# Two more Strassen pairs in the second feed-forward half, with weight sums made in DRAM by transfers

## The chip, the cores and the metric

The kernel runs on one core of a Trainium2 chip. The metric is the device time of one execution in microseconds (us), as the median of three runs. Five engines work side by side, each through its own queue in order: PE (TensorE, matmuls; PEld is its weight load), DVE (VectorE), ACT (ScalarE), POOL (GpSimd) and SP (SyncE, which here only issues transfers). Weights come from DRAM by transfers that share 16 DMA engines.

## The reference

One decoder layer on 512 tokens of width 1024, in float32: a feed-forward half, a mixer (attention beside a state-space model), and a second feed-forward half. What the change touches is the last of these, with an inner width of 2816:

```python
def rms_norm(x, g):
    xf = x.astype(jnp.float32)
    y = xf * lax.rsqrt(jnp.mean(xf * xf, axis=-1, keepdims=True) + NORM_EPS)
    return (y * g.astype(jnp.float32)).astype(x.dtype)

def swiglu(x, w_in, w_out):
    gate, up = jnp.split(x @ w_in, 2, axis=-1)
    return (jax.nn.silu(gate) * up) @ w_out

h = rms_norm(x, ffn1_pre_g[l])
x = x + 0.5 * rms_norm(swiglu(h, ffn1_w_in[l], ffn1_w_out[l]), ffn1_post_g[l])
...
h = rms_norm(x, ffn2_pre_g[l])
x = x + 0.5 * rms_norm(swiglu(h, ffn2_w_in[l], ffn2_w_out[l]), ffn2_post_g[l])
```

The factor of `rms_norm` for one token (called r below) is a scalar per token. So r may be applied before or after the product with `w_in`.

## The kernel before, in words

**Precision.** Each float32 operand is split into a high half (`xh`, `whi`, `ah`; made by ACT, L117, L163, L166) and a low half (`xl`, `wlo`, `al`; the difference, made by DVE or POOL, L119, L164, L167). Each product is three matmuls, high by high, high by low, low by high (`mm3`; all matmuls are recorded on L144).

**Tiles of the inner width.** 2816 is 22 tiles f of 128. Each f has a gate tile and an up tile, each a product of 1024x128 weights with 1024x512 inputs. A *standard* f (`products`) takes 2 x 8 x 3 = 48 matmuls of 128x512, tiles `gu`. A *pair* (`pair`, two neighbouring f at once) sees the weights as four blocks a11, a12, a21, a22 (a first index of 2 is the up part, a second index of 2 is the second half of the 1024 rows), and the inputs as four blocks of 4 x 256 columns. Seven products of 24 matmuls of 128x256 give what eight would give (the scheme of Strassen and Winograd). It needs four sums of weight blocks, c3 = a11 + a21, c2 = c3 + a22, c1 = a21 + a22 and c4 = c2 + a12, made by DVE (L609), and sums of input blocks, n1, n2, t3, t4, made once. The products go into the banks `wx`, `wy`, `wq`.

`NSTD` says how many f of each half are standard: 8 in the first half, 6 in the second. Of the 6, the first two (tiles `first`) are computed in the boundary.

**Weights.** SP issues each load (`wraw`, `wa`, `wx`; 512 KB), ACT makes the high half, DVE or POOL the low half. Three `wraw` buffers and four buffers for each half rotate.

**Boundary.** Between two stages `boundary` applies the norm to the residual x. It goes by token halves h = 0, 1: the last products of the stage before (`yt`), then `prep(h, k)` for each of eight row tiles (new x, its `xh` and `xl`, and the square, which POOL adds to `acc`, L178), and `begin(h, k)`, the first matmuls of the next stage (tile `first`). PE sums the squares of the first token half over partitions with `st` in the middle of the second half's `begin`, and of the second half later, in the next stage (`late`); DVE makes `nv` from it and POOL the power r (L207). The first boundary leads from feed-forward to the mixer, the second from the mixer to the second feed-forward half.

**Second half before.** `swiglu_half`: f = 2 to 5 are standard, with eight token transposes of x spread between their matmuls (`xt`, L505, copied out of PSUM by ACT on L507 and stored to DRAM for the end). The input blocks are scaled by the gain and r (L533, 16 ops), then summed and split (`sums`). Eight pairs follow, f = 6 to 20, with the output products `outp` between them; `finish` ends with the last output products and the last norm, tile by tile.

**Order.** Matmuls, transfers marked by `dma` and operations marked by `fix` keep the order of the program. The rest is ordered by the scheduler of the framework on each engine's queue. Semaphores hold an instruction until its operands are ready, and everything behind it on the same engine waits too.

Of the kernel before, what the change touches and what calls it, by code (L numbers as in the profile page):

```python
# [17 lines left out]
P = 128  # L18
# [11 lines left out]
NSTD = (8, 6)  # L30
# [14 lines left out]
class Layer:  # L45
# [30 lines left out]


# [195 lines left out]
    def boundary(self, y, tail, ipost, half, inext, chunks):  # L273
# [40 lines left out]
        def prep(h, k, fix=lambda i: i):  # L314
# [5 lines left out]
            self.split(xh(k)[:, hs[h]], xl(k)[:, hs[h]], xk, self.g(inext, k), fix)  # L320
            self.sq_acc(acc2[:, hs[h]], xk, k == 0, nc.gpsimd)
# [46 lines left out]
        for k in range(KD):  # L368
            if k > 1:
                prep(0, k, fx if k > 5 else lambda i: i)  # L370
            begin(0, k)
            if k == 2:
                post[1][0](late, fix=fx)
            if k == 4:
                rr[1] = post[1][1]()
        for k in range(KD):
            prep(1, k)
            begin(1, k)
            if k == 3:
                pre[0][0](fixp=fx)  # L380
            if k == 6:
                pre[0][1]()
        self.xh, self.xl = xh, xl
# [6 lines left out]
    def ffn(self, n, first, scope):  # L390
# [42 lines left out]
        def outp(i, ms=range(KD), tails=None, hold=0):  # L433
# [3 lines left out]
            def part(m, k0, k1):  # L437
# [15 lines left out]
                else:  # L453
                    nc.vector.tensor_tensor(out=y(m), in0=b[m], in1=y(m), op=ALU.add)
# [20 lines left out]
        prep = sums(True)  # L475
# [5 lines left out]
        for m in range(2, KD):  # L481
# [3 lines left out]
            outp(0, (m,))  # L485
        for f in range(NSTD[0], NF, 2):
# [24 lines left out]
    def seven(self, fin, w_in, ig, r, ah, al):  # L511
# [13 lines left out]
        def sums(early=False):  # L525
# [13 lines left out]
            more[0] = (yield) or fin  # L539
            if early:  # L540
                self.pad(more[0], 192)
# [4 lines left out]
            bh, bl = [self.b16(n, F32R) for n in ("bh", "bl")] if early else (None, None)  # L546
            v = lambda t, i: t.rearrange("p (q k) c -> p q (k c)", q=4)[:, i]

            def plain(*ts):
                for t in ts:  # L550
                    i = len(blocks)
                    blocks.append((v(bh, i), v(bl, i)))
                    self.split(*blocks[i], t)

            if early:
                plain(b11)
            V.scalar_tensor_tensor(out=n2, in0=n1, scalar=-1.0, in1=b22, op0=ALU.mult, op1=ALU.subtract)
            if early:
                plain(b21)
# [6 lines left out]
            if early:  # L566
                plain(b22, n1)
# [4 lines left out]
            if not early:  # L572
                yield
                bh, bl = [self.b16(n, F32R) for n in ("bh", "bl")]
                plain(b11, b21, b22, n1)
            yield

        def block(f, up, kh):
            if up:
                t = wx() if kh else more[0].tile([P, 1024], F32, name="wa", tag="wa")  # L580
# [6 lines left out]
        def cut(t, pool=False):  # L587
            hi, lo = self.halves(True)
# [3 lines left out]
        def times(bank, w, xb, first, parted=False):  # L592
            for g in range(2):
# [914 lines left out]
```

## Time and profile before

| What | Value |
|---|---|
| runs, us | 918.75, 918.01, 916.20 (median 918.01) |
| profiled execution, us | 916.19 |
| its span, us | 914.2 |
| PE busy | 98% of the span |
| DVE busy | 72% |
| ACT busy | 48% |
| POOL busy | 24% |
| the 16 DMA engines, main queue | 34.5% |

Busy shares are means over stages that differ. Matmul ends are modelled in the records, so the time of one matmul is read from start to start. A row of groups gives busy time, then the mean of one in ns, then the idle time of the engine ahead of it and what ended that. A row of the timeline gives start, duration, engine, line and operation, output and inputs, form and count, and in brackets the wait ahead of it.

### The profile page before, as it was taken

The numbers are of one execution on the slowest core, as the hardware profiler recorded it, in microseconds if no ns is written. First come the engines' busy times: TensorE is split into PE (matmuls) and PEld (weight loads), VectorE is DVE, ScalarE is ACT, GpSimd is POOL, SyncE is SP. The second block draws the span as 40 slices with busy tenths as digits, with TensorE's granted clock in tenths as the row PEclk, the third lists the DMA queues.
The fourth block names the chain that finished last, engine by engine and source line by source line (L and its number), as shares of the span: only waits on it lengthen the run. The fifth ranks groups of instructions, "written<-read, shape, count | busy, mean of one in ns | idle before, by whom it ended". The sixth has DMA issues, their size and how long they took to land.

```text
span 914.2 us, 15367 instructions
## 1 busy us (share of the span) xinstructions
PE 898.9 (98%) x6169; PEld 801.4 (88%) x6169; DVE 656.0 (72%) x1071; ACT 442.0 (48%) x685; POOL 217.5 (24%) x127
## 2 busy tenths in 40 slices
PE   9999999999999999999999999999999999999996
PEld 7787789998999989978777889888899989998995
DVE  6999786755678666758898567898368557855756
ACT  6263763553355543525745654573355514541542
POOL 0423301322123134500000025523222222221321
PEclk9999999999999999999999999999999999999999
DMA  8223662334231262283321452145222422332222
GB/s 277 94 70 115 196 248 76 107 102 137 77 119 61 68 194 86 92 221 109 116 70 51 153 167 71 29 179 180 97 93 99 133 92 93 116 116 92 92 93 92
DMA packets 47734, 106.81 MB, mean 117 GB/s; under 512 B 7824, under 2 KB 11152, under 8 KB 47120
## 3 DMA queue, kind: packets, MB, share of 16 engines
q1 hardware_dynamic: 46080, 102.21, 34.5%
q10 hardware_dynamic: 1584, 3.63, 1.1%
q8 instruction: 48, 0.79, 0.3%
q14 instruction: 22, 0.18, 0.1%
HBM read 96.13 MB, written 9.70 MB: 116 GB/s over the span
## 4 chain that ended last, share of the span: by engine, by line
PE 79%; DVE 6%; issue 2%; DMA 2%; ACT 1%; POOLq 0%; POOL 0%; DVEq 0%; SPq 0%; ACTq 0%
PE yo L144 21%; PE wx L144 18%; PE wq L144 9%; PE yt L144 6%; PE wy L144 4%; PE gu L144 4%; PE prj L144 4%; PE first L144 3%; PE prv L144 2%; PE mo L144 2%; PE ys L144 1%; PE st L144 1%; DMA w1d<-w1s 1%; PE pt L1098 1%; PE sc L144 1%
## 5 line engine op out<-in xcount | busy, mean ns | idle before, releaser
L117 ACT CAST whi<-wraw 128x1024 fp32r<-128x1024 f32 (+5 forms) x128 | 124.0, 976 | 160.3 <-PE yo L144 65.5
L119 POOL TENSOR_TENSOR wlo<-wraw,whi 128x1024 fp32r<-128x1024 f32 (+1 forms) x41 | 109.2, 2666 | 297.6 <-ACT whi L117 290.3
L119 DVE TENSOR_TENSOR wlo<-wraw,whi 128x1024 fp32r<-128x1024 f32 (+5 forms) x87 | 107.4, 1242 | 75.7 <-ACT whi L117 75.6
L144 PE MATMUL wx<-tq,whi 128*128 128x256 f32 x720 | 124.7, 276 | 0.0
L144 PEld LDWEIGHTS wx<-tq,whi 128*128 128x128 f32 x720 | 108.3, 188 | 0.0
L119 DVE TENSOR_TENSOR wlo<-wsum,whi 128x1024 fp32r<-128x1024 f32 x60 | 73.6, 1227 | 46.5 <-ACT whi L117 46.4
L117 ACT CAST whi<-wsum 128x1024 fp32r<-128x1024 f32 x60 | 63.0, 1050 | 81.8 <-PE yo L144 28.1
L144 PE MATMUL wx<-tq,wlo 128*128 128x256 f32 x360 | 99.4, 276 | 0.0
L119 POOL TENSOR_TENSOR wlo<-wx,whi 128x1024 fp32r<-128x1024 f32 x15 | 41.5, 2764 | 176.3 <-ACT whi L117 128.5
L144 PEld LDWEIGHTS wx<-tq,wlo 128*128 128x128 f32 x360 | 67.6, 188 | 0.0
L144 PE MATMUL gu<-xh,whi 128*128 128x512 f32 x168 | 67.2, 400 | 0.0
L144 PE MATMUL gu<-xh,wlo 128*128 128x512 f32 x168 | 65.7, 391 | 1.1 <-POOL wlo L119 1.1
L144 PE MATMUL wq<-bh,whi 128*128 128x256 f32 x240 | 66.2, 276 | 0.0
L144 PE MATMUL wq<-bl,whi 128*128 128x256 f32 x240 | 66.2, 276 | 0.0
L144 PE MATMUL wq<-bh,wlo 128*128 128x256 f32 x240 | 66.2, 276 | 0.0
L144 PE MATMUL gu<-xl,whi 128*128 128x512 f32 x168 | 65.5, 390 | 0.0
L144 PE MATMUL yo<-ah,whi 128*128 128x512 f32 x144 | 56.3, 391 | 0.0
L144 PE MATMUL yo<-al,whi 128*128 128x512 f32 x144 | 56.1, 389 | 0.0
L144 PE MATMUL yo<-wlo,ah 128*128 128x512 f32 x144 | 56.0, 389 | 0.0
L144 PE MATMUL yo<-whi,ah 128*128 128x512 f32 x144 | 56.0, 389 | 0.0
L144 PE MATMUL yo<-ah,wlo 128*128 128x512 f32 x144 | 56.0, 389 | 0.0
L144 PE MATMUL yo<-whi,al 128*128 128x512 f32 x144 | 56.0, 389 | 0.0
(267 smaller groups left out, 2385.0 us busy)
## 6 DMA issues: line engine op xcount, KB each, us to landing
wraw<-w1i SPq DMA_DIRECT2D x28, 512.0 KB, 3.7
wraw<-w2i SPq DMA_DIRECT2D x28, 512.0 KB, 3.6
wraw<-w2o SPq DMA_DIRECT2D x18, 512.0 KB, 3.7
wraw<-wmi SPq DMA_DIRECT2D x12, 512.0 KB, 4.1
wraw<-w1o SPq DMA_DIRECT2D x8, 512.0 KB, 4.2
wa<-w2i SPq DMA_DIRECT2D x8, 512.0 KB, 3.7
wx<-w2i SPq DMA_DIRECT2D x8, 512.0 KB, 4.0
wa<-w1i SPq DMA_DIRECT2D x7, 512.0 KB, 3.6
```

The costliest lines, as they stand in the source:

```text
L117: fix(self.nc.scalar.copy(out=hi, in_=raw))
L119: fix(eng.tensor_tensor(out=lo, in0=raw, in1=hi.bitcast(F32), op=ALU.subtract))
L144: i = self.nc.tensor.matmul(*a, **k)
L1098: self.fix(nc.tensor.transpose(b[i][:, o:o + P], sc[:, c:c + P], self.ident))
```

## The change

- `NSTD` of the second half goes from 6 to 2: f = 2 to 5 become two more pairs, so ten pairs run, f = 2 to 20.
- The sums of weight blocks of these ten pairs no longer come from DVE. `block_sums` makes them in DRAM: for each pair two copies of blocks, two accumulating transfers (c3, c1), a copy of c3 to c2, an accumulate, a copy of c2 to c4, an accumulate. Copies are issued by SP, accumulates by POOL, each 512 KB, 80 in all. A step of it is taken by `self.more()` at places in the first half: after standard f, between output products, six in each pair, and eight in the first boundary. A pair of the second half then loads seven blocks.
- The input blocks of the second half are not scaled by r. In the second boundary ACT writes gain times x into the buffer `ymix` and DVE makes n1 and n2 from it by 256 columns (`wide_sums`); t3 and t4 follow inside pair 2. The plain blocks are taken straight from `xh` and `xl`.
- DVE multiplies the gate of a pair by r ahead of the silu. The up part stays unscaled, and the result y is scaled by r in `finish` (in the square by ACT and in the gain by DVE).
- The transposes `xt` stand between products of pair 2: one in the boundary's wake, two, then five.

```diff
-NSTD = (8, 6)
+NSTD = (8, 2)
+    def block_sums(self):
+        nc, w = self.nc, self.a["w2i"]
+        src = lambda f, up, kh: w[f + NF * up:f + NF * up + 2, :, kh * S:(kh + 1) * S].rearrange("f p c -> p f c")
+        fs = range(NSTD[1], NF, 2)
+        self.csum = {(f, c): self.dr.tile([P, 2, S], F32, name=f"c{c}_{f}") for f in fs for c in (3, 1, 2, 4)}
+        copy = lambda o, i: self.dma(out=o, in_=i)
+        plus = lambda o, i: self.fix(nc.gpsimd.dma_start(out=o, in_=i, accum_op=ALU.add))
+        stages = (lambda f, t: copy(t(3), src(f, 0, 0)), lambda f, t: copy(t(1), src(f, 1, 0)),
+                  lambda f, t: plus(t(3), src(f, 1, 0)), lambda f, t: plus(t(1), src(f, 1, 1)),
+                  lambda f, t: copy(t(2), t(3)), lambda f, t: plus(t(2), src(f, 1, 1)),
+                  lambda f, t: copy(t(4), t(2)), lambda f, t: plus(t(4), src(f, 0, 1)))
+        turns = ((0, 1), (2, 3), (4,), (5,), (6,), (7,))
+        for n in range(len(fs) + len(turns) - 1):
+            for j in range(len(turns) - 1, -1, -1):
+                if 0 <= n - j < len(fs):
+                    f = fs[n - j]
+                    for i in turns[j]:
+                        stages[i](f, lambda c: self.csum[f, c])
+                        yield
...
@@ def boundary
             self.split(xh(k)[:, hs[h]], xl(k)[:, hs[h]], xk, self.g(inext, k), fix)
+            if wide:
+                fix(nc.scalar.activation(out=t, in_=xk, func=AF.Copy, scale=self.g(inext, k)))
...
             begin(0, k)
+            self.more()
...
             begin(1, k)
+            if wide and k:
+                wide(k - 1)
...
@@ def ffn
                 products(f)
+                self.more(2 + (f > 2))
...
             outp(0, (m,))
+            self.more()
...
@@ def pairs
+        def whole(f, c):
+            t = wsum()
+            nc.sync.dma_start(out=t, in_=csum[f, c].rearrange("p f c -> p (f c)"))
+            return t
...
+            then = lambda i: hooks[i]() if i in hooks else None if csum else self.more()
...
+            if csum:
+                c2 = whole(f, 2)
+            else:
+                a21, a22 = block(f, 1, 0), block(f, 1, 1)
+                c3 = wsum()
+                add(a11, a21, c3)
+                c2 = wsum()
+                add(c3, a22, c2)
...
             V.tensor_tensor(out=half(gt, 1), in0=p2(Q), in1=p2(s2), op=ALU.add)
+            if csum:
+                V.tensor_tensor(out=gt, in0=gt, in1=r.unsqueeze(1).to_broadcast([P, 2, S]), op=ALU.mult)
             nc.scalar.activation(out=gt, in_=gt, func=AF.Silu)
...
@@ def wide_sums
+            if k < 4:
+                V.tensor_tensor(out=h(k, 0), in0=h(k, 0), in1=h(k, 1), op=ALU.subtract)
+            else:
+                V.scalar_tensor_tensor(out=self.n2[:, (k - 4) * HT:(k - 3) * HT], in0=h(k - 4, 0), scalar=-1.0, in1=h(k, 1),
+                                       op0=ALU.mult, op1=ALU.subtract)
...
@@ def swiglu_half
+        def begun():
+            blocks[3] = put(3, part(gx, 0, 0))
+            step(2)
+
+        def further():
+            third()
+            late[0]()
+            step(2)
+
+        def last():
+            fourth()
+            step(5)
+
+        pair(2, hooks={0: begun, 1: further, 2: late[1], 3: last}, into=(room(2), room(1)))
...
@@ def finish
+            fx(V.scalar_tensor_tensor(out=yg[b, i], in0=at(y, b, i), scalar=r4[:, b:b + 1], in1=self.gt[d][:, sl],
+                                      op0=ALU.mult, op1=ALU.mult))
```

Line numbers in the rows of the changed kernel are its own: L87 is an accumulating transfer, L163 a copy (all transfers of `dma` have this line), L146 a weight load, L201 the add of a square (L178 before), L230 the power (L207 before), L142 a low half, L541 a transpose.

First place: POOL in the first boundary. Before, from the power of the first token half on:

```order
L178 TENSOR_TENSOR acc<-acc,sq 128x256
L207 TENSOR_TENSOR p_3571<-nv,mhalf 128x2
L178 TENSOR_TENSOR acc<-acc,sq 128x256 x8
L207 TENSOR_TENSOR r_3565<-nv,mhalf 128x2
L178 TENSOR_TENSOR acc<-acc,sq 128x256 x4
```

Now, from the same add (`c_20_345` is c2 of the pair f = 20, `c_20_346` its c4, `c_18_342` c4 of f = 18):

```order
L201 TENSOR_TENSOR acc<-acc,sq 128x256
L230 TENSOR_TENSOR p_3684<-nv,mhalf 128x2
L201 TENSOR_TENSOR acc<-acc,sq 128x256
L87 DMA c_20_345<-w2i 256x1x512
L201 TENSOR_TENSOR acc<-acc,sq 128x256
L87 DMA c_18_342<-w2i 256x1x512
L201 TENSOR_TENSOR acc<-acc,sq 128x256 x2
L87 DMA c_20_346<-w2i 256x1x512
L201 TENSOR_TENSOR acc<-acc,sq 128x256 x4
L230 TENSOR_TENSOR r_3678<-nv,mhalf 128x2
```

Three accumulating transfers now stand among the adds; the one into c4 of pair 20 stands ahead of the seventh add of the first token half.

Second place: SP at the same time, with what each row waits for (DMASW are POOL's transfers, DMAHW SP's own):

```order
L163 DMA c_20_345<-c_20_343 16x8192 [waits DMASW0_49]
L163 DMA c_18_342<-c_18_341 16x8192 [waits DMASW3_49]
L146 DMA wraw<-wmi 128x1024 [waits DMAHW0_49,Pool_49]
L146 DMA wraw<-wmi 128x1024 [waits DMAHW1_49,DVE_49]
L146 DMA wraw<-wmi 128x1024 [waits DMAHW2_49,Pool_49]
L1163 DMA bias<-bias 128x512 [waits PE_49]
L1163 DMA bias<-bias 128x512
L163 DMA c_20_346<-c_20_345 16x8192 [waits DMASW5_49]
```

The last row is the copy of c2 to c4 for pair 20; it waits for POOL's accumulate into c2, and loads of the mixer stand in the same queue.

Third place: DVE at the end of the second boundary (`xl` is the low half of the input, `n_6292` the block sum n2, `tq<-wraw` the low half of the first weight block of pair 2, L760 makes a sum for t3):

```order
L190 SCALAR_TENSOR_TENSOR xl<-x,sm,xh 128x256
L728 SCALAR_TENSOR_TENSOR n_6292<-ymix 128x256
L187 TENSOR_TENSOR tq<-ymix,tq 128x1024
L190 SCALAR_TENSOR_TENSOR xl<-x,sm,xh 128x256
L728 SCALAR_TENSOR_TENSOR n_6292<-ymix 128x256
L760 TENSOR_TENSOR ymix<-ymix 128x4x256
L142 TENSOR_TENSOR tq<-wraw,tq 128x1024
L187 TENSOR_TENSOR tq<-n_6292,tq 128x1024
L142 TENSOR_TENSOR wlo<-wsum,whi 128x1024 x2
```

Before, the last `xl` was followed by `nv` and the scaled blocks, and the low half of the first weight had been made ahead of it, inside the boundary.

More of the change, by code (lines that the diff above doesn't have):

```diff
@@ L271, in start, with boundary @@
         return o, r4, r, self.rstd(acc, r4, r)
-    def boundary(self, y, tail, ipost, half, inext, chunks):
+    def boundary(self, y, tail, ipost, half, inext, chunks, wide=None):
         nc = self.nc
@@ L571, in sums, with pairs @@
             self.split(*tq[2], t4)
[L572 to L575, printed above, removed]
             yield
+        room = lambda: more[0].tile([P, 1024], F32, name="wa", tag="wa")
+        return sums, self.pairs(w_in, blocks, tq, wsum, gp, (room, wx), r, ah, al)
+    def pairs(self, w_in, blocks, tq, wsum, gp, rooms, r, ah, al, csum=None):
+        nc, V = self.nc, self.nc.vector
+        wa, wx = rooms
         def block(f, up, kh):
-            if up:
-                t = wx() if kh else more[0].tile([P, 1024], F32, name="wa", tag="wa")
+            if up and not csum:
+                t = wx() if kh else wa()
             else:
@@ L605, in keep, with pair @@
             return t
-        def pair(f, lead=False, late=False):
-            (b11, b21, b22, n1), (n2, t3, t4) = blocks, tq
+        def pair(f, lead=False, late=False, hooks={}, into=(None, None)):
             add = lambda x, z, t: V.tensor_tensor(out=t, in0=x, in1=z, op=ALU.add)
@@ L699, in outp @@
                         V.tensor_tensor(out=y(b, d), in0=b4[b], in1=y(b, d), op=ALU.add)
-        sums, pair = self.seven(fin, w_in, 4, r, ah, al)
-        for f in range(NSTD[1]):
-            if f >= len(o0) // 2:
-                products(f)
-            if f == 2:
-                hidden(0)
-                hidden(1)
-            if f >= 2:
-                hidden(f)
-            if f == 3:
-                for _ in hook:
-                    pass
-                rest = sums()
-                for _ in range(7):
-                    next(rest)
-        next(rest)
+        tq[0] = put(0, n2)
+        pair = self.pairs(w_in, blocks, tq, lambda: fin.tile([P, 1024], F32, name="wsum", tag="wsum", bufs=3),
+                          lambda: fin.tile([P, 1024], F32, name="gp", tag="gp", bufs=2), (None, None), r, ah, al, self.csum)
+        def begun():
[9 more added lines that the diff above has]
+        pair(2, hooks={0: begun, 1: further, 2: late[1], 3: last}, into=(room(2), room(1)))
+        hidden(0)
+        hidden(1)
         self.gt = [self.acct() for _ in range(2)]
@@ L722, in swiglu_half @@
         outp(0)
-        for f in range(NSTD[1], NF, 2):
-            pair(f, f in (NSTD[1], 12, 18), f == NF - 2)
+        for f in range(6, NF, 2):
+            pair(f, f in (6, 12, 18), f == NF - 2)
             if f in (10, 16):
@@ L1430, in run @@
         first = self.start(chunks, ipre)
+        back = self.block_sums()
+        self.more = lambda n=1: [next(back, None) for _ in range(n)]
         for p, q in zip(parts, parts[1:] + " "):
@@ L1439, in run @@
                 if p != "g":
-                    first = self.boundary(*out, *post[p], *nxt[q])
+                    first = self.boundary(*out, *post[p], *nxt[q], self.wide_sums if q == "g" else None)
 _SHAPES_OUT = (S, D)
```

135 lines of the change are left out of this document (81 added, 54 removed).

## The prediction

> **What bounds the kernel now.** I read the page's busy times and chain first, then the wait view of PE, then windows by stage, then single rows where the change puts something new.
>
> ```profile
> PE 898.9 (98%) x6169; PEld 801.4 (88%) x6169; DVE 656.0 (72%) x1071; ACT 442.0 (48%) x685; POOL 217.5 (24%) x127
> ...
> PE idle L144 <- DVE pp L848: 1.2, 1, 1.2
> PE xt L505 <- DVE nv L205: 1.2, 1, 1.2
> PE gu L144 <- POOL wlo L119: 1.1, 1, 1.1
> ...
> PE first L144 <- DVE xl L167: 0.7, 3, 0.3
> ```
>
> TensorE is busy for 98% of the span, and its longest single wait is 1.2 us. So two things count: how many matmuls there are, and whether an edit makes PE wait where it does not wait now. No row of the wait view names a DMA: weights always arrive in time. A faster DVE, ACT or POOL is worth nothing by itself; a late one costs what PE waits.
>
> **Fewer matmuls.** Rows of PE's timeline (start, duration, then engine, line and tile) and two windows (length, busy time and count of each engine, clock, DMA share, GB/s):
>
> ```profile
> 607.16 0.39 PE L144 MATMUL gu<-xh,whi 128*128 128x512 f32 x1
> ...
> 616.00 0.39 PE L144 MATMUL gu<-xh,whi 128*128 128x512 f32 x1
> ...
> 240.00:316.00 76.00, 76.00 (x672) 75.96 (x671) 56.09 (x56) 40.73 (x47) 17.94 (x7) 1.00 0.24 77
> 316.00:338.00 22.00, 22.00 (x101) 18.27 (x101) 14.87 (x18) 9.99 (x12) 4.80 (x2) 1.00 0.60 188
> 572.00:600.00 28.00, 26.60 (x182) 23.82 (x181) 23.02 (x41) 12.88 (x27) 12.81 (x11) 1.00 0.29 93
> ...
> 667.00:724.00 57.00, 57.00 (x504) 56.99 (x503) 38.72 (x39) 31.80 (x37) 15.51 (x6) 1.00 0.31 103
> ```
>
> The two `gu` rows are 39 starts apart: 8.84 / 39 = 0.227 us for a 128x512 matmul. The window from 667 us is three pairs: 57.00 / 504 = 0.113 us for a 128x256 one. Four standard tiles of 48 matmuls take 4 x 48 x 0.227 = 43.5 us; the two pairs in their place take 2 x 168 x 0.113 = 38.0 us. **Term 1: -5.5 us.** It is firm to 0.2 us, since the granted clock is 1.00 in all of these windows.
>
> **DVE work that leaves.** Four weight sums a pair go, and one multiplication of the gate by r comes in.
>
> ```profile
> L119 DVE TENSOR_TENSOR wlo<-wraw,whi 128x1024 fp32r<-128x1024 f32 (+5 forms) x87 | 107.4, 1242 | 75.7 <-ACT whi L117 75.6
> L609 DVE TENSOR_TENSOR wsum<-wsum,wx 128x1024 f32<-128x1024 f32 x15 | 24.6, 1638 | 0.3
> L609 DVE TENSOR_TENSOR wsum<-wraw,wa 128x1024 f32<-128x1024 f32 x15 | 18.3, 1222 | 10.0 <-DMA wraw<-w2i 9.4 <-DMA wraw<-w1i 0.5
> ```
>
> That is about 5.5 us less and 1.2 us more per pair of 19 us. In the window of three pairs DVE is busy for 38.72 of 57.00 us and PE waits for nothing, so the work was covered: 0 us. The unscaled input blocks (16 scaled ops, the splits of four blocks) also lay beside PE: 0 us.
>
> **The second boundary's end.** PE's second half of `first` now runs straight into product one of pair 2. DVE owes it the low half of that weight block.
>
> ```profile
> 562.28 1.21 DVE L119 TENSOR_TENSOR tq<-wraw,tq 128x1024 fp32r<-128x1024 f32 x1
> ...
> 580.84 0.48 DVE L167 SCALAR_TENSOR_TENSOR xl<-x,sm,xh 128x256 fp32r<-128x256 f32 x1 [0.58 <-ACT xh L166]
> ...
> 583.47 0.28 PE L144 MATMUL first<-xl,whi 128*128 128x256 f32 x1
> ...
> 584.72 0.40 PE L144 MATMUL gu<-xh,tq 128*128 128x512 f32 x1
> ```
>
> Before, the low half of the first weight was made at 562.28, well ahead of 584.72, and the last `xl` was ready 2.2 us before PE took it at 583.47. The change puts seven 256-column ops (about 0.4 us apart) and a 1.21 us split ahead of the last `xl`, and takes the split of 562.28 away: 2.8 us more, 0.6 us of it in the idle time, so `xl` lands about when PE wants it. Behind it stand a 256-column op (0.5), a 128x1024 one (1.2) and only then the low half (1.2): 2.9 us, against 1.5 us until PE's third matmul of the product. **Term 2: +1.4 us** (0 if `xl` keeps its lead, 2.0 if it slips further). The 16 unscaled copies on ACT fall into ACT's gaps: ACT is busy for 12.88 of 28 us from 572 us on. The wait of `xt` for `nv` (1.2 us above) stays: `nv` now stands behind a sum and the splits instead of behind scaled ops. I count it as equal.
>
> **Transposes in a row.** Eight token transposes were spread over products; now five stand together.
>
> ```profile
> 603.50 0.60 PE L505 MATMUL xt<-ident,x 128*128 128x128 f32 x4
> 603.86 0.48 PE L144 MATMUL gu<-xh,whi 128*128 128x512 f32 x1
> ...
> 598.01 0.59 ACT L507 COPY xt<-xt 128x512 f32<-128x512 f32 x1 [1.50 <-PE xt L505]
> ```
>
> Four transposes hold PE for 0.36 us and ACT's copy takes 0.59 us. Their work was paid before too. Five in a row outrun ACT by 4 x 0.23 = 0.9 us, and free banks decide whether PE feels it: **term 3: +0.9 us** (0 with banks enough, 1.5 when the first copy also waits behind a cast).
>
> **The end.** Gate times r stands between the last gate sum and its silu.
>
> ```profile
> 882.69 0.69 DVE L638 TENSOR_TENSOR gp<-wq,kp 128x512 f32<-128x512 f32 x1 [1.96 <-PE wq L144]
> 883.41 1.06 ACT L639 ACTIVATE gp<-gp 128x1024 f32<-128x1024 f32 x1 [2.50 <-DVE gp L638]
> 884.51 0.69 DVE L644 SCALAR_TENSOR_TENSOR gp<-kp,gp 128x512 f32<-128x512 f32 x1 [1.13 <-ACT gp L639]
> 885.24 0.62 ACT L163 CAST ah<-gp 128x512 fp32r<-128x512 f32 x1 [0.76 <-DVE gp L644]
> 886.02 1.46 DVE L164 TENSOR_TENSOR al<-gp,ah 128x512 fp32r<-128x512 f32 x2
> ...
> 887.05 0.39 PE L144 MATMUL yt<-whi,al 128*128 128x512 f32 x1
> ```
>
> The chain is serial: sum, silu, product, split. It gets 1.22 us longer, and the first `al` (done at 886.75) was 0.3 us ahead of PE at 887.05. **Term 4: +0.8 us** (0.5 to 1.2). Scaling y at the end rides on ops that are there already.
>
> **Eighty transfers.** The sums of ten pairs are made in the first half by 40 copies (SP) and 40 accumulating transfers (POOL), each 512 KB and DRAM to DRAM.
>
> ```profile
> q1 hardware_dynamic: 46080, 102.21, 34.5%
> ...
> wraw<-w1i SPq DMA_DIRECT2D x28, 512.0 KB, 3.7
> w1d<-w1s SPq DMA_DIRECT2D x8, 256.0 KB, 4.4
> w2d<-zb SPq DMA_DIRECT2D x2, 1024.0 KB, 5.2
> ...
> 563.52 0.34 SPq L123 DMA_DIRECT2D wraw<-w2i  x1
> ```
>
> 102.21 MB kept all 16 engines busy for 34.5% of 914.2 us, so 512 KB hold them for 1.6 us. Six transfers come in each first-half pair. Three copies at 1.6 us and three accumulates at 1.6 (one copy's worth) to 3.2 (two) make 9.7 to 14.5 us in 19 us, beside the 0.24 of window 240 to 316: a share of 0.75 to 1.0. It just fits, and the sums are not needed before 585 us: 0 us, with a tail upward (rival C). In the second half a pair loads 7 x 512 KB instead of 4: 11.3 of 19 us. 0 us.
>
> The queue is the nearer danger. In the first boundary POOL has the adds of the squares, which PE awaits for `st`, and in their midst stand accumulates that wait for earlier transfers.
>
> ```profile
> 368.00 0.71 POOL L207 TENSOR_TENSOR p<-nv,mhalf 128x2 f32<-128x2 f32 x1 [2.37 <-DVE nv L205]
> 368.68 4.78 POOL L178 TENSOR_TENSOR acc<-acc,sq 128x256 f32<-128x256 f32 x5
> ...
> 379.28 0.50 PE L144 MATMUL st<-ones,acc 128*128 128x2 f32 x4
> ...
> L119 POOL TENSOR_TENSOR wlo<-wraw,whi 128x1024 fp32r<-128x1024 f32 (+1 forms) x41 | 109.2, 2666 | 297.6 <-ACT whi L117 290.3
> ```
>
> POOL finished these adds at 373.5, PE needs them at 379.28: 5.8 us of slack. In the new order the accumulate into c2 of tile 20 goes out after one add (369.6); its landing releases SP's copy c2 to c4; that landing releases POOL's accumulate into c4, and the seventh add stands behind it. The chain is 369.6 + accumulate + copy + POOL's issue + 0.95 for the add. An accumulate lands in 4.4 (the shorter DRAM row) to 9.4 us (two copies of 4.7, between the DRAM rows), a copy in 3.7 to 5.2, and an issue holds POOL for 0.4 (SP's row) to 2. That gives 379.05 to 387.2, so PE waits 0 to 7.9 us. I take 5.5, 4.7 and 0.7, nearer to the DRAM rows than to their double: 381.5. **Term 5: +2.2 us.** Elsewhere POOL idles ahead of its low halves, waiting for ACT (297.6 us over 41 of them, last row), so an issue of a us or two is absorbed.
>
> By the Trainium skill (Collectives: The Full Stack, section "The bandwidth ceiling: the fold count and why AG ≠ RS ≠ AR") a reducing transfer reads two sources and runs at about half a copy's rate. The trace of before holds no accumulate to set beside it; by that rule the accumulate lands at the upper bound and term 5 is near +5.7 us.
>
> **Sum.** -5.5 + 1.4 + 0.9 + 0.8 + 2.2 = -0.2 us. The profiled execution took 916.2 us and would take 916.0; the median shown, 918.0, lies 1.8 us above it, so I forecast 917.8 us.
>
> **Rivals.**
> A, the transfers are cheap: an accumulate lands like the 4.4 us copy, term 5 is 0, and banks hide the transposes. -5.5 + 1.4 + 0.8 = -3.3: 914.7 us. For it: POOL is 24% busy and the slack is 5.8 us. Against it: two dependent DRAM trips in that slack. The Trainium skill ("DMA: Bandwidth & Descriptors", section "Anatomy of one DMA — SWDGE (gpsimd) path") fits 2.0 us plus bytes over 436 GB/s, an estimate of 3.2 us here, which would make this the case; no run shows it yet.
> B, POOL's queue holds PE in the first boundary: slower, from the point where accumulate, copy and issue together exceed 8.7 us (379.28 - 369.6 - 0.95). At 9.4 + 4.7 + 0.7 the wait is 6.1 us; the sum is +3.7: 921.7 us. For it: the order of the queue; against it: a few us less in any of three durations undo it.
> C, backlog: an accumulate that costs 5 us of all engines makes 3 x 6.6 + 0.24 x 19 = 24.4 us of transfers per 19 us pair. Seven pairs overflow by 38 us; as an estimate a third reaches PE through SP's and POOL's queues, which carry weights and low halves too: about +12, 930 us. For it: window 316 to 338 is at 0.60 already; against it: no PE wait on a DMA today.
> D, second-half loads bind: a new block waits for its buffer and costs about 1 us a pair for ten pairs: 928 us. Against it: 11.3 of 19 us.
>
> **Numbers.** Forecast 0.35 (own range 915 to 921), A 0.33, B 0.16, C 0.11, D 0.05. A change under 0.3% (2.75 us) can't be told from none. Faster is A: 0.33. Slower is B, C and D and little of the forecast's edge: 0.33; the rest, 0.34, is no change. The range runs from A with its stalls smaller still (912) over B to the edge of C and D (928).
>
> **What would show it.** Right: 192 fewer 128x512 and 336 more 128x256 matmuls at 0.227 and 0.113 us; new PE waits of about 1.4 us at the first product (for `tq` from DVE), under 1 us at the five `xt`, 0.8 us at `yt`, and 2 us at `st` of the first boundary with POOL as its releaser. Wrong: an accumulate that lands in over 8 us or under 4.5, PE waits on a DMA or a POOL low half between 70 and 340 us, or waits on `wsum` loads in the second half.

## The result, and the profile after

The changed kernel takes 991.85 us (median of four runs, 991.34 to 993.50) against 917.36 us for the kernel before (four runs): a ratio of 1.0814, with a 95% interval of 1.0793 to 1.0836. It is slower by 8%, far outside the range of 912 to 928 us that was forecast. The profiled execution took 991.34 us, 75.2 more than that of before.

From the page of the changed kernel: the engines' busy times, POOL's DMA queue, the group of POOL's accumulating transfers (busy time, mean ns of one, idle time ahead of them and what ended it) and transfers (count, size, median us from issue to landing):

```profile
PE 921.7 (93%) x6313; PEld 825.9 (83%) x6313; DVE 635.9 (64%) x1036; ACT 455.0 (46%) x706; POOL 247.7 (25%) x167
...
q0 software_dynamic: 10880, 20.97, 13.6%
...
L87 POOL DMA_DIRECT2D c<-w2i x40 | 42.6, 1064 | 181.3 <-issue 132.6
...
c<-w2i POOLq DMA_DIRECT2D x40, 512.0 KB, 7.6
...
wraw<-w1i SPq DMA_DIRECT2D x28, 512.0 KB, 5.7
```

PE fell from 98% to 93% of a longer span, yet its busy time rose by 22.8 us, although the new pairs need less of it: PE waited, and it also ran slowly for a while. POOL is busy for only 25%, but it stood idle for 181.3 us just ahead of its 40 accumulates, 132.6 of them with no cause that the profile names. Loads of first-half weights (`wraw`) land in 5.7 us instead of 3.7.

The wait view of PE (us in total, times, longest):

```profile
PE wx L167 <- POOL wlo L142: 26.2, 6, 7.3
PE kc L1120 <- ACT kt L1116: 6.0, 1, 6.0
PE st L167 <- POOL acc L201: 5.7, 1, 5.7
PE xt L541 <- ACT xt L543: 3.9, 2, 2.8
PE wx L167 <- DVE tq L142: 2.5, 1, 2.5
PE gu L167 <- DVE wlo L142: 2.4, 1, 2.4
```

Two of the three largest have POOL as the releaser: low halves of first-half weights, and the squares of the first boundary. Where the time went, by the starts of PE's first matmul of each stage (us, profiled executions):

| stage | before | change | larger scratch (experiment 2) | no sums (experiment 1) |
|---|---|---|---|---|
| to the first output products | 103.9 | +3.0 | +3.6 | -0.7 |
| first output products | 46.3 | +12.4 | +4.8 | +0.1 |
| first-half pairs, with their output products | 188.0 | +39.4 | 0.0 | 0.0 |
| first boundary | 47.8 | +10.3 | +5.2 | 0.0 |
| mixer | 148.8 | +0.6 | +1.0 | +0.8 |
| second boundary | 50.0 | +0.6 | -0.1 | 0.0 |
| second half, to its last output products | 300.5 | +7.3 | +8.8 | +6.3 |
| end | 21.8 | +0.9 | +1.0 | +1.0 |

The third, the wait for `kt`, lies in the first output products, at 117 us. So 65 of 75 us were lost where the transfers are issued, in the first four rows, and 8 in the second half and the end.

**How POOL loses it.** POOL's timeline in one first-half pair of the changed kernel (start, duration, instruction; in brackets the idle time ahead):

```profile
163.73 1.06 POOL L87 DMA_DIRECT2D c<-w2i  x1
172.55 1.05 POOL L87 DMA_DIRECT2D c<-w2i  x1 [7.76 <-issue]
181.69 1.06 POOL L87 DMA_DIRECT2D c<-w2i  x1 [8.09 <-DVE wlo L142]
182.27 2.86 POOL L142 TENSOR_TENSOR wlo<-wx,whi 128x1024 fp32r<-128x1024 f32 x1
```

The view of the accumulates' line gives the time from issue to landing (shortest, median, longest): for all 40, for the one of 163.73 alone, and for the one of 172.55 alone.

```profile
DMA to landing us min/median/max: 5.8/7.6/11.2
...
DMA to landing us min/median/max: 8.5/8.5/8.5
...
DMA to landing us min/median/max: 8.8/8.8/8.8
```

163.73 + 8.5 = 172.2, and the next accumulate is issued at 172.55; 172.55 + 8.8 = 181.35, and the next at 181.69. Never are two in flight, and 32 of the 39 successors were issued within 0.5 us of the landing before. The low halves stand behind the waiting accumulate. The same timeline at 207 us, and then PE's:

```profile
207.76 1.04 POOL L87 DMA_DIRECT2D c<-w2i  x1 [5.13 <-DVE wlo L142]
208.34 2.94 POOL L142 TENSOR_TENSOR wlo<-wx,whi 128x1024 fp32r<-128x1024 f32 x1
```

```profile
211.33 0.58 PE L167 MATMUL wx<-tq,wlo 128*128 128x256 f32 x1 [6.02 <-POOL wlo L142]
```

PE waits 6.02 us for a low half that takes 2.94 us to make. The name behind the arrow at 207.76 is an inference of the profile; the landing times are what fits.

**And then PE runs at half speed.** Windows of the changed kernel (length, PE busy and matmuls, granted clock, DMA share, GB/s), around that wait; then over four pairs, with busy time and count of all five engines ahead of the clock:

```profile
205.00:211.30 6.30, 0.31 (x3) 0.71 0.68 183
211.30:214.60 3.30, 3.27 (x15) 0.51 1.06 192
214.60:220.00 5.40, 5.40 (x50) 1.00 0.92 291
```

```profile
274.00:371.00 97.00, 83.01 (x675) 82.22 (x674) 63.56 (x57) 40.59 (x48) 29.92 (x19) 0.91 0.76 179
```

After the wait PE is granted half the clock for 3.3 us: 15 matmuls, where the next 5.4 us hold 50. Over four pairs, 76.00 us before, PE is idle for 14.0 us and busy for 7.0 us more with the same number of matmuls (675, 672 before): each us of waiting here cost another half us in clock. The Trainium skill (TensorE: Matmul & The Clock Gate, section "🔬 Part 1: The HAM clock gate (the "warmup" mystery)") says that the array falls to half rate when idle and needs about 3.4 us of work to be released; the 3.3 us of this window agree.

### The profile page after: what moved, and what is told of

It is laid out like the page before. It is cut to its first block, busy times and chain, and to the rows that moved or that the text cites. A ratio compares the mean times of both kernels' runs of the same rounds, so it can differ in the third digit from the quotient of the medians.

```text
span 989.3 us, 15844 instructions
## 1 busy us (share of the span) xinstructions
PE 921.7 (93%) x6313; PEld 825.9 (83%) x6313; DVE 635.9 (64%) x1036; ACT 455.0 (46%) x706; POOL 247.7 (25%) x167
## 3 DMA queue, kind: packets, MB, share of 16 engines
q0 software_dynamic: 10880, 20.97, 13.6%
## 4 chain that ended last, share of the span: by engine, by line
PE 48%; DVE 7%; issue 3%; ACT 2%; DMA 2%; POOL 1%; POOLq 0%; DVEq 0%; ACTq 0%
PE yo L167 12%; PE wx L167 11%; PE wq L167 6%; PE yt L167 5%; PE prj L167 3%; PE prv L167 2%; PE wy L167 2%; PE mo L167 2%; PE ys L167 1%; PE st L167 1%; DVE x L342 1%; DVE xl L190 1%; PE pt L1195 1%; PE sc L167 1%; PE pv L167 1%
## 5 line engine op out<-in xcount | busy, mean ns | idle before, releaser
L142 POOL TENSOR_TENSOR wlo<-wraw,whi 128x1024 fp32r<-128x1024 f32 (+1 forms) x48 | 122.1, 2554 | 363.3 <-ACT whi L140 359.8
L142 DVE TENSOR_TENSOR wlo<-wraw,whi 128x1024 fp32r<-128x1024 f32 (+5 forms) x85 | 101.7, 1202 | 118.1 <-ACT whi L140 117.7
L167 PE MATMUL wx<-tq,whi 128*128 128x256 f32 x816 | 152.5, 289 | 0.7 <-ACT kp L649 0.5
L167 PE MATMUL wx<-tq,wlo 128*128 128x256 f32 x408 | 118.9, 291 | 26.2 <-POOL wlo L142 26.2
L167 PEld LDWEIGHTS wx<-tq,whi 128*128 128x128 f32 x816 | 131.3, 200 | 1.3 <-ACT kp L649 1.3
L142 DVE TENSOR_TENSOR wlo<-wsum,whi 128x1024 fp32r<-128x1024 f32 x68 | 92.2, 1358 | 46.1 <-ACT whi L140 45.9
L87 POOL DMA_DIRECT2D c<-w2i x40 | 42.6, 1064 | 181.3 <-issue 132.6
L167 PE MATMUL gu<-xh,wlo 128*128 128x512 f32 x112 | 43.9, 392 | 2.4 <-DVE wlo L142 2.4
L167 PE MATMUL first<-xh,whi 128*128 128x256 f32 (+1 forms) x144 | 43.8, 304 | 1.1 <-ACT xh L189 0.8
L167 PE MATMUL first<-xl,whi 128*128 128x256 f32 (+1 forms) x144 | 43.6, 303 | 1.2 <-DVE xl L190 0.9
L167 PE MATMUL gu<-xh,whi 128*128 128x512 f32 x112 | 44.7, 399 | 0.0
L167 PE MATMUL gu<-xl,whi 128*128 128x512 f32 x112 | 43.6, 390 | 0.0
L167 PE MATMUL first<-xh,wlo 128*128 128x256 f32 (+1 forms) x144 | 42.4, 295 | 0.0
```

Source lines behind the costliest of these rows:

```text
L87: plus = lambda o, i: self.fix(nc.gpsimd.dma_start(out=o, in_=i, accum_op=ALU.add))
L142: fix(eng.tensor_tensor(out=lo, in0=raw, in1=hi.bitcast(F32), op=ALU.subtract))
L167: i = self.nc.tensor.matmul(*a, **k)
```

## The experiments

Two theories stood at the start. The *queue theory*: an accumulate issued by POOL holds POOL until the one before has landed, and what is queued behind it reaches PE late. The *traffic theory*: the transfers fill the 16 DMA engines, and weights arrive late. A third, the *SP theory*, has SP's copies wait in SP's queue for landings, with weight loads standing behind them. Each experiment edits the changed kernel; its ratio is to the kernel before, with a 95% interval. Figures per stage are the difference to before of the stage in the table above.

**1. No sums in DRAM.** The 80 transfers go, and with them the sums; the second half loads plain weight blocks in their place, in the same number and size.

```diff
-        for n in range(len(fs) + len(turns) - 1):
+        for n in range(0):
...
-            nc.sync.dma_start(out=t, in_=csum[f, c].rearrange("p f c -> p (f c)"))
+            src = w_in[f + NF * up:f + NF * up + 2, :, kh * S:(kh + 1) * S].rearrange("f p c -> p f c")
+            nc.sync.dma_start(out=t.rearrange("p (f c) -> p f c", f=2), in_=src)
```

> Leaves out all 80 transfers that make the block sums; the second half loads seven plain weight blocks a pair (so the sums are missing from what it computes). Baseline for every theory: the first 386 us should go as in the kernel before (the transfers cost +65 us there: 3.0 up to the first output products, 12.3 in these, 39.5 in the pairs, 10.3 in the first boundary), so about 926 us. What is left over the 917 us of before (about +9: a sum of -5.5 and stalls in pair 2 and at the end) then belongs to the second half and not to the transfers. If the second half's stalls were caused by late DRAM writes, it would be below 918.

Measured: 923.62 us, 1.0065 (1.0048 to 1.0082). Every first-half stage is back within 0.8 us of before; the second half stays at +6.3. So the transfers cost 68 of the 74.5 us, and the second half has a loss of its own. Its largest waits on PE are these:

```profile
PE xt L541 <- ACT xt L543: 4.0, 2, 2.9
PE wx L167 <- DVE tq L142: 2.4, 1, 2.4
```

Behind the wait for `tq` stand these rows of DVE's timeline, and of POOL's at the same time:

```profile
582.48 0.96 DVE L190 SCALAR_TENSOR_TENSOR xl<-x,sm,xh 128x256 fp32r<-128x256 f32 x1
...
585.93 1.75 DVE L142 TENSOR_TENSOR tq<-wraw,tq 128x1024 fp32r<-128x1024 f32 x1
```

```profile
581.24 5.35 POOL L201 TENSOR_TENSOR acc<-acc,sq 128x256 f32<-128x256 f32 x4
```

The order is the one forecast, but these ops take half as long again or twice as long (1.75 instead of 1.21 us, 0.96 instead of 0.48) while POOL adds squares beside it.

**2. A larger scratch for POOL's transfers.** The program sets one size, 1024, for the scratch of transfers that POOL issues; in the kernel before POOL issues none.

```diff
-    nc = bacc.Bacc("TRN2", target_bir_lowering=False, num_devices=1, dynamic_dma_scratch_size=1024)
+    nc = bacc.Bacc("TRN2", target_bir_lowering=False, num_devices=1, dynamic_dma_scratch_size=3072)
```

> Only the scratch space for descriptors of POOL's transfers goes from 1024 to 3072 bytes a partition; same instructions. Queue theory (each accumulate waits on POOL until the one ahead has landed, because the scratch holds one, and low halves stand behind it): the 8 us gaps between successive accumulates vanish, and most of the first half's 65 us with them: 925 to 950 us. Traffic theory (the 16 engines are full, shares 0.74 to 1.00, and all lands late): no gain, 980 to 1000 us. SP theory (copies wait in SP's queue for landings, weight loads stand behind them): 960 to 985 us.

Measured: 942.88 us, 1.0281 (1.0257 to 1.0305), 49.0 us faster than the change. POOL's timeline now has up to four accumulates issued back to back:

```profile
303.88 4.25 POOL L87 DMA_DIRECT2D c<-w2i  x4
```

The window over four pairs, all engines, and the landing of all 40 accumulates:

```profile
241.00:317.00 76.00, 76.00 (x639) 74.71 (x638) 55.95 (x54) 39.05 (x45) 33.33 (x21) 1.00 0.93 225
```

```profile
DMA to landing us min/median/max: 6.3/10.2/17.2
```

PE is busy for all of the 76.00 us, at a DMA share of 0.93, where the change lost 21 us at 0.76. Transfers now land later than in the change (10.2 us against 7.6), and it costs nothing there. That refutes the traffic theory for the first-half pairs and bears the queue theory out; the 960 to 985 us of the SP theory did not come either.

In the first boundary 5.2 us are left. There the chain of term 5 shows by itself: POOL's accumulate into c4 is released by SP's copy of c2 (POOL's timeline). The accumulate into c2 had landed after 6.4 us and the copy after 4.1, and PE waits 2.4 us for `st`.

```profile
389.45 1.05 POOL L87 DMA_DIRECT2D c<-w2i  x1 [6.49 <-DMA c<-c]
```

**3 and 4. Plain copies instead of accumulates** (the additions are left out), issued by POOL with the scratch of 1024, or by SP. First experiment 3, then 4:

```diff
-        plus = lambda o, i: self.fix(nc.gpsimd.dma_start(out=o, in_=i, accum_op=ALU.add))
+        plus = lambda o, i: self.fix(nc.gpsimd.dma_start(out=o, in_=i))
```

```diff
-        plus = lambda o, i: self.fix(nc.gpsimd.dma_start(out=o, in_=i, accum_op=ALU.add))
+        plus = lambda o, i: self.dma(out=o, in_=i)
```

> The 40 accumulating transfers are issued by POOL as plain copies (the additions are left out), scratch 1024 as in the change. Queue theory: still one at a time, each held until the one ahead has landed, but that is shorter (5 us instead of 7.6): 945 to 970 us. Traffic theory: the share of the engines falls by 40 x 1.7 us, most stalls go: 925 to 945 us. If plain copies do not wait for one another at all, the wait belongs to accumulating and not to the scratch.

> The 40 accumulating transfers become plain copies issued by SP (the additions are left out), so POOL's queue holds none of the 80, and the traffic is that of 80 copies, as in the run with POOL's plain copies. Queue theory: POOL's low halves are in time and the time is 925 to 940 us. Traffic theory: equal to the run with POOL's plain copies. SP theory: SP's queue, now with all waits for landings, keeps weight loads late: 950 us or more.

Measured: 930.32 us, 1.0144 (1.0124 to 1.0164) from POOL; 932.10 us, 1.0163 (1.0143 to 1.0184) from SP. From experiment 3, two rows of POOL's timeline, the landing of all 40 copies, and POOL's queue on the page (packets, MB, share of 16 engines):

```profile
299.12 2.01 POOL L87 DMA_DIRECT2D c<-w2i  x3
304.14 0.65 POOL L87 DMA_DIRECT2D c<-w2i  x1 [3.01 <-PE wx L167]
```

```profile
DMA to landing us min/median/max: 3.9/6.7/9.5
```

```profile
q0 software_dynamic: 5760, 20.97, 6.9%
```

Under the same scratch three copies are issued in 2.01 us, without waiting for each other. A fourth one close behind them does wait: the first landed after 4.7 us, at 303.8, and the fourth was issued at 304.14. The time of experiment 3 is below the 945 to 970 us that the queue theory expected, which had each copy wait for the one ahead; so the theory is narrowed to how much of the scratch a transfer takes up. That of experiment 4 lies within its 925 to 940. There, all 80 copies in SP's queue leave the first-half pairs at 0.0, against the 950 us or more of the SP theory. An accumulate has 10880 / 40 = 272 packets against 5760 / 40 = 144 of a copy, and holds the 16 engines for 13.6% x 989.3 / 40 = 3.36 us against 6.9% x 927.2 / 40 = 1.60. The Trainium skill's rule that the prediction cited (Collectives: The Full Stack, the same section: a reduce at half a copy's rate, stated there for ring collectives) agrees in its size: 2.1 times.

**5. No sums, and the transposes spread again** over the products of pairs 2 and 4 (experiment 1, with this).

```diff
-            step(2)
...
-            step(5)
+            step()
...
-        pair(2, hooks={0: begun, 1: further, 2: late[1], 3: last}, into=(room(2), room(1)))
+        pair(2, hooks={0: begun, 1: further, 2: late[1], 3: last, 4: step, 5: step}, into=(room(2), room(1)))
...
-        pair(4)
+        pair(4, hooks={i: step for i in range(5)})
```

> As the run without sum transfers (923.6 us; the sums left out), but the eight token transposes stand one at a time: four between products of pair 2, four of pair 4, instead of 1, 2 and 5. Theory: the two waits of the five in a row for ACT's copy (1.3 + 3.1 us), and the stretch at half clock behind them (2.3 + 0.6 us), come from the bunching: 916 to 918 us, with no PE wait of xt over 0.5 us. Rival: the clock falls for another reason (the change to 128x256 matmuls): the waits go, the stretch at clock 0.5 stays, about 919.5 us. Second rival: ACT is late by itself: no gain, 923 us.

Measured: 916.52 us, 0.9991 (0.9982 to 1.0000); the second half is at -1.4 instead of +6.3. The waits for `xt` are gone, and with them what followed. The windows of PE in experiment 1 (behind the waits for `tq` and for `xt`) and then in experiment 5 (the same places):

```profile
587.00:591.00 4.00, 3.27 (x16) 0.62 0.00 0
...
611.00:615.00 4.00, 4.00 (x21) 0.50 0.53 198
```

```profile
587.00:592.00 5.00, 3.89 (x33) 1.00 0.07 16
600.00:620.00 20.00, 20.00 (x179) 1.00 0.63 218
```

Of the 7.7 us between the two second halves, 4.0 are the waits for `xt`, 2.0 the clock behind them (4 us at 0.50), and 1.5 the clock behind the first product (4 us at 0.62), which experiment 5 keeps at 1.00 although PE waits for `tq` there too (2.5 us). Why it does is open.

**6. A scratch of 2048.**

```diff
-    nc = bacc.Bacc("TRN2", target_bir_lowering=False, num_devices=1, dynamic_dma_scratch_size=1024)
+    nc = bacc.Bacc("TRN2", target_bir_lowering=False, num_devices=1, dynamic_dma_scratch_size=2048)
```

> As the change, descriptor scratch 2048 bytes instead of 1024 (3072 gave 942.9). Queue theory: two accumulates fit, the third of three in a row waits on POOL for the first to land: between 943 and 992 us, nearer to 943, about 950 us, and gaps ahead of every third accumulate only. If the scratch merely has a threshold for a single transfer (any size above 1024 frees all), 943 us.

Measured in one run, without an interval: 943.83 us, about as with 3072. But this is not a threshold for a single transfer. POOL's timeline has, at the place where 3072 lets four accumulates out at once (the row in experiment 2):

```profile
306.03 3.18 POOL L87 DMA_DIRECT2D c<-w2i  x3
313.28 1.04 POOL L87 DMA_DIRECT2D c<-w2i  x1 [4.07 <-DVE al L187]
```

Three fit, not two as the queue theory had expected. The fourth waits for the first, which landed after 6.9 us: 306.03 + 6.9 = 312.9. Of the 40 accumulates it is the only one issued like this behind a landing, so the smaller limit costs next to nothing. The limit thus grows with the scratch. At 1024 three copies fit (3 x 144 = 432 packets), and two accumulates (2 x 272 = 544) do not; at 2048 three accumulates (816) fit and four (1088) do not; at 3072 five (1360) were in flight in experiment 12. A limit of 454 to 543 packets for each 1024 of scratch would explain all of these. What the scratch counts is not in any record, so this is an inference.

**7. Sums by transfers for the two new pairs alone.** 16 transfers, spread over the first half and none in the boundary; the other eight pairs make their sums on DVE as before; the transposes spread.

```diff
-        fs = range(NSTD[1], NF, 2)
+        fs = (2, 4)
...
+        when = {0: (2, 0), 2: (2, 1), 5: (2, 2), 6: (4, 0), 8: (4, 1), 9: (2, 3), 11: (2, 4), 13: (4, 2), 17: (4, 3),
+                19: (4, 4), 21: (2, 5), 25: (4, 5), 26: (2, 6), 30: (2, 7), 31: (4, 6), 36: (4, 7)}
```

The calls of `more` in the first boundary, between the first output products and after the standard tiles go too; those inside the first-half pairs stay, and the other eight pairs have their buffers of before again.

> Sums by transfers for pairs 2 and 4 only (16 of the 80, one or two per first-half pair, each accumulate at least four products behind the one ahead); DVE makes those of the other eight pairs as before; transposes one at a time; the first weight block of pair 2 goes to a buffer that is free early, so its halves are made inside the boundary; n1's halves go where the unused input block lies. Queue theory: so few accumulates never wait for one another, the first half takes its 386 us as before. With the waits for tq (2.6 us and 1.5 at half clock) and xt (7 us in all) gone, the second half takes 300.5 - 5.5 + 0 to 2 us: 912 to 915 us against 917.3. If DVE (68% busy in the pairs, 1.2 us more per pair) binds, 918 to 925 us.

Measured: 915.62 us, 0.9977 (0.9967 to 0.9988). It beats the change and, by 0.2%, the kernel before, but stays just above the 912 to 915 us that were expected. First half and first boundary are untouched (0.0 or -0.1 each), the second half gains 4.4 us, and the second boundary gives 3.5 back. Its waits on PE:

```profile
PE first L166 <- DVE xl L189: 2.9, 4, 1.2
PE first L166 <- ACT xh L188: 1.4, 1, 1.4
```

**8. The boundary alone.** Experiment 5, with only those transfers that the change issues in the first boundary (and three copies that they need).

```diff
+        at = 0
...
-                        stages[i](f, lambda c: self.csum[f, c])
+                        if at in (30, 36, 42):
+                            g, c = {30: (16, 4), 36: (20, 3), 42: (18, 2)}[at]
+                            copy(self.csum[g, c], src(g, 0, 0))
+                        if at > 72:
+                            stages[i](f, lambda c: self.csum[f, c])
+                        at += 1
```

> As the run without sum transfers and with spread transposes (916.5 us), but the last seven transfers stay, those of the first boundary, in the change's order on POOL and SP, scratch 1024 (three plain copies ahead of it give them something to read; all other sums are left out). It prices term 5 alone. My term's formula: accumulate (5.5) + copy (4.7) + issue, PE waits about 2 us at st: 918 to 919. With the queue theory: four accumulates one behind the other, each held until the one ahead has landed (about 5 us each without other traffic), before the seventh add: the wait is 5 to 8 us, and half-clock time follows: 923 to 927 us. If the boundary's +10 us came from the backlog of the pairs instead, no change: 916.5.

Measured: 927.22 us, 1.0111 (1.0092 to 1.0129); the first boundary takes 10.8 us more, and every other stage is within 1.5 us of experiment 5. POOL's timeline in the boundary:

```profile
371.15 1.10 POOL L87 DMA_DIRECT2D c<-w2i  x1 [1.26 <-ACT sq L205]
...
377.40 1.06 POOL L87 DMA_DIRECT2D c<-w2i  x1 [4.38 <-issue]
...
384.88 1.08 POOL L87 DMA_DIRECT2D c<-w2i  x1 [4.86 <-issue]
```

The largest wait on PE, behind which the granted clock is 0.50 from 388 to 390 us:

```profile
PE st L173 <- POOL acc L207: 4.6, 1, 4.6
```

The accumulates landed after 6.0 and 7.2 us; 371.15 + 6.0 and 377.40 + 7.2 are the starts of the next ones to 0.3 us. The prediction's formula had given 918 to 919 us, the queue theory 923 to 927.

**9, 10 and 11. Three tries for the second boundary** of experiment 7. In 9 (`two_pairs_late`) the block sums n1 and n2 move behind the boundary; in 10 (`two_pairs_mixed`) only n2 does; in 11 (`two_pairs_ordered`) they go behind the first product, with the first block's split and the boundary's last row tile pinned in program order on every engine.

The core of 9 and 11, then of 10, then of 11 alone:

```diff
-            if wide and k:
-                wide(k - 1)
```

```diff
-            if wide and k:
+            if wide and 0 < k < 5:
                 wide(k - 1)
```

```diff
-            prep(1, k)
+            prep(1, k, fx if k == 7 else lambda i: i)
...
-            times(X, cut(a11, into=into[0]), blocks[0], True, lead)
+            times(X, cut(a11, into=into[0], fix=self.fix if into[0] else lambda i: i), blocks[0], True, lead)
```

> As the run with sums for pairs 2 and 4 (915.6), whose second boundary was 3.5 us longer, for the low halves of the input came late behind 8 half ops on DVE. Here n1 and n2 are two whole ops behind the boundary's last low halves, and the sums t3 and t4 are held behind the splits of the third product. If DVE's order in the boundary is the cause: boundary back to 50 us, pair 2 with 0 to 1.5 us of waits: 912 to 914 us. If the boundary is late for ACT's sixteen extra ops instead: 915 to 916.

> As the run before it, but n1's four half ops stay in the boundary (DVE has less behind it, more inside): boundary 1 to 2 us longer, nothing waits in pair 2: 913 to 915 us. It loses to the run before it if DVE's order inside the boundary is what counts, and wins if pair 2 is the tighter place.

> As the run with n1 and n2 behind the boundary (916.5 us, whose second boundary was still 3 us longer: the low half of pair 2's first weight and n1 stood inside it). Here nothing is added on DVE before the boundary's last low half; behind it stand, held in this order, the low half of the first weight, n1, n2, the splits of n2, c2, n1, c1, and only then t3 and t4. If DVE's order decides: the boundary takes 50 us as before, the first product waits 0.3 to 1 us, the third 0 to 1: 912 to 914.5 us. If the boundary stays 3 us longer, the cause is not DVE's order but the extra ops on ACT: 916.

Measured: 916.49 us, 0.9995 (0.9985 to 1.0005); 917.93 us, 1.0015 (1.0005 to 1.0025); 931.05 us, 1.0146 (1.0124 to 1.0168). None helps, and none of the expected times came. In 9 the boundary still takes 3.0 us more: the scheduler put n1 (L785) in front of the last `xl` again (DVE's timeline), and pair 2 has a new wait of 1.4 us for a DVE low half.

```profile
580.73 1.22 DVE L785 TENSOR_TENSOR ymix<-ymix 128x1024 f32<-128x1024 f32 x1
...
581.94 0.47 DVE L189 SCALAR_TENSOR_TENSOR xl<-x,sm,xh 128x256 fp32r<-128x256 f32 x1
```

In 11 the pin held on ACT too and put the last `xh` behind a copy that waits for PE; DVE's last `xl` followed it at 589.01 us (ACT's timeline):

```profile
588.20 0.37 ACT L237 COPY rs<-rp 128x256 f32<-128x256 f32 x1 [3.51 <-PE rp L166]
588.47 0.51 ACT L188 ACTIVATE xh<-x,sm 128x256 fp32r<-128x256 f32 x1
```

So 11 says nothing on the order it was meant to test. Most of its loss lies behind the boundary: the second half takes 8.7 us more than before, with several waits (2.4 us for an ACT high half) and a mean clock of 0.84 from 600 to 632 us.

The second boundary takes 3 to 4.5 us more in the versions with two pairs, and only 0.6 us more in the change. Neither rival of the expectations, n1 and n2 on DVE or ACT's extra ops, names what the traces of 7, 9 and 10 show: there the first two weight blocks of pair 2 are split inside the boundary, where the change makes these low halves behind it. Experiment 7, POOL's timeline and then DVE's:

```profile
571.18 2.37 POOL L141 TENSOR_TENSOR tq<-wx,tq 128x1024 fp32r<-128x1024 f32 x1
```

```profile
571.32 2.52 DVE L189 SCALAR_TENSOR_TENSOR xl<-x,sm,xh 128x256 fp32r<-128x256 f32 x1
```

Beside POOL's low half, `xl` takes 2.52 instead of 0.47 us, and PE waits 1.2 us for it; POOL's power `p`, beside DVE's low half, takes 1.64 instead of 0.71, and PE waits 0.8. That would be 2.0 of the 3.5 us. No run moves these splits alone, so it is not shown, and the rest is open.

**12. All 80 transfers, moved.** Scratch of 3072, none in the boundary, eight in a first-half pair instead of six, transposes spread as in experiment 5. The call of `more` in the first boundary goes:

```diff
             begin(0, k)
-            self.more()
...
-            then = lambda i: hooks[i]() if i in hooks else None if csum else self.more()
+            then = lambda i: hooks[i]() if i in hooks else None if csum else self.more(1 + (i in (1, 4)))
```

> All 80 transfers and the whole computation stay; scratch 3072; none of the transfers in the first boundary (eight instead of six in each first-half pair); transposes one at a time as in the runs before. Sum of the pieces measured apart: 942.9 - 5.2 (boundary) - about 8 (transposes, with their half clock) = 929 to 931 us. Against that: the first half's pairs had a DMA share of 0.93 with six transfers each, and eight ask for 1.2 of what the 16 engines can do; if that backlog reaches PE, the pairs grow again by 5 to 20 us: 935 to 950. If the engines' fullness hides altogether because the sums are not urgent: 925 to 931.

Measured: 934.61 us, 1.0192 (1.0175 to 1.0209), just under the 935 to 950 us of a backlog that reaches PE. The boundary is at 0.0 and the second half at -1.8, but the pairs are at +14.1. Two windows in the pairs with all engines, five accumulates in POOL's timeline, and the loads of one weight block:

```profile
160.00:207.00 47.00, 42.00 (x366) 41.41 (x364) 35.84 (x31) 22.85 (x27) 18.87 (x12) 1.00 1.02 277
...
241.00:317.00 76.00, 71.18 (x557) 68.06 (x557) 59.97 (x52) 35.37 (x39) 33.40 (x21) 1.00 0.95 244
```

```profile
272.92 5.33 POOL L87 DMA_DIRECT2D c<-w2i  x5
```

```profile
wa<-w1i SPq DMA_DIRECT2D x7, 512.0 KB, 9.5
```

Here weights land late by traffic: a load of `wa` takes 9.5 us from its issue (5.0 in experiment 2). PE loses 5.0 of 47 us at a share of 1.02 and 4.8 of 76 at 0.95, where experiment 2 lost nothing at 0.93. So the share alone does not tell the limit; the transfers also stand closer together, up to five accumulates in a row. SP's queue may add to it: from 150 to 330 us it stood for 70.4 us ahead of copies that waited for accumulates (56.2 in experiment 2), with loads behind them, and no run parts the two. In this arrangement 80 such transfers don't fit into the pairs beside their own weights.

## Why the prediction was wrong

By experiments 1 to 3 the 74.5 us come apart like this: the second half's own loss +6.3 (to 923.6), 40 copies by SP and 40 by POOL +6.7 (930.3), accumulates in place of POOL's copies +12.6 (942.9, with room in the scratch), waiting for each other +49.0 (991.9).

- **"0 us" for the eighty transfers** is the step that failed. The sum of engine time was nearly right: 3 x 1.6 + 3 x 3.36 = 14.9 us per pair is just above the 9.7 to 14.5 that were worked out, and "it just fits" holds in experiment 2. But "an issue of a us or two is absorbed" counted POOL's issue (1.06 us measured) as the whole hold. With a scratch of 1024 an accumulate held POOL until its predecessor landed, 7.6 us from issue in the median, and the slack ahead of POOL's low halves did not cover several in a row: +39.4 in the pairs. Of the +12.4 in the first output products 6.0 are the wait for `kt`, which has another way: ACT makes it from a transfer of SP (`w1d`) that lands late; with the larger scratch 4.0 of it are still there, with plain copies from POOL 0.5.
- **Term 5** (the boundary) had the right place, wait and releaser, and was too small: 2.2 forecast, 5.7 waited (4.6 in experiment 8), 10 to 11 us for the stage. The formula let an accumulate of another pair cost an issue; the three stood one after another, and the half clock came on top. The chain itself was right: in experiment 2, where accumulates do not wait for each other's room, it binds, and PE waits 2.4 us for `st`. That this is near the 2.2 forecast is partly luck, since the accumulate took longer than assumed (6.4 instead of 5.5) and the copy less (4.1 instead of 4.7). For an accumulate at the upper bound the prediction has 5.7 us in one place and 6.1 in rival B; its sum gives 6.1.
- **Term 1** (fewer matmuls) is borne out in kind: the page counts 144 more matmuls (6313 against 6169), as 336 - 192 gives, and the second half gains 4.4 and 4.8 us in experiments 7 and 9, though their second boundary gives 3.5 and 3.0 back.
- **Term 2**: right in place and releaser, 1.4 forecast, 2.4 to 2.5 measured, with DVE's ops at up to twice their time while POOL was adding. **Term 3**: right place, 0.9 forecast; 4.0 of wait and 2.0 of clock measured. **Term 4**: 0.8 forecast, 0.3 to 0.4 of wait at `yt`; the end as a whole takes 0.9 to 1.0 more.
- **The rivals.** A's cheap accumulate (4.4 us) did not come: the shortest landed in 5.8. B and C each named part of the mechanism: POOL's queue, and a backlog that reaches PE through it. But C's cause was an accumulate that costs all engines 5 us; it was 3.36, and PE lost time at a share of 0.76 and none at 0.93. Late loads do cost PE in experiment 12, at 0.95 and 1.02. D did not occur: no wait on a second-half load.
- **The signs to look for** were the right ones: PE waits on a POOL low half in the first half were named as what would prove the forecast wrong.

Open: 3 to 5 us before the first output products, in every version with all 80 transfers (PE waits 2.4 to 5.0 us there for a DVE low half, with loads landing later); and whether `w1d` for `kt` is late by traffic or in SP's queue, where copies wait for accumulates.

## What to carry to other kernels

A transfer's cost is not its engine time alone: ask what it holds on the engine that issues it, and count what stands behind it in that queue. An engine at 25% busy can be the bound; its idle time ahead of an instruction (here 181.3 us ahead of 40 issues) tells it, and one run with a larger scratch parts a queue from traffic. A wait of PE can cost more than its length, so many small operations are better spread than stood together.

## What was not expected of the hardware

- Accumulating transfers from POOL went out one at a time with a scratch of 1024, at most three with 2048 and up to five with 3072; of plain copies three were in flight with 1024. The next one holds POOL until one of them has landed, with all that stands behind it.
- A 512 KB accumulate from DRAM to DRAM landed in 5.8 to 11.2 us with nothing of its kind beside it, a copy from POOL in 3.9 to 9.5 with up to three in flight. The Trainium skill's fit (DMA: Bandwidth & Descriptors, "Anatomy of one DMA — SWDGE (gpsimd) path"), from which the prediction's estimate of 3.2 us came, lies below both.
- PE at half clock for 3 to 4 us after waits of 2.4 to 6 us. It isn't automatic: PE kept full clock after a wait of 2.5 us in experiment 5 and, for `kt`, of 3.4 us in experiment 12 (granted clock 1.00 from 112 to 119 us).
- DVE ops of 1.21 us took 1.75 beside POOL's adds, and one of POOL's low halves of 2.66 us (mean) took 3.36.
